# Seven-product up-projections on one core: split order, places, squares and token sums rearranged

## The chip, the core and the metric

The kernel runs on one core of one Trainium2 chip. The metric is the device time of one execution in microseconds (us); the number of a kernel is the median of its runs. TensorE (PE) does the matmuls, VectorE (DVE), ScalarE (ACT) and GpSimd (POOL) the elementwise work, and SyncE (SP) issues most transfers. Each engine works through its own list of instructions in order and waits on semaphores of the others.

## The reference, cut to what matters

The whole program is a chain of layers over 512 tokens of width 1024, in single precision. The change concerns the two squared-ReLU MLPs (width 4096):

```python
def sqrelu_mlp(h, w_up, w_down):
    u = jax.nn.relu(h @ w_up)
    return (u * u) @ w_down

def first_block(...):
    for i in range(DEPTH):                       # DEPTH = 2
        h = rms_norm(x, mixer_norm[i])
        ...                                      # attention (i = 0), rwkv (i = 1)
        x = x + sqrelu_mlp(rms_norm(x, mlp_norm[i]), mlp_w_up[i], mlp_w_down[i])
    return rms_norm(x, final_norm)
```

After them come two SwiGLU layers and a mixer, which the change does not touch.

## The kernel before

Activations lie as eight tiles `x[m]` of 128 features x 512 tokens. A single-precision product is made of three fast ones (`mm3`, lines 454 to 456): every operand is split into a high part `hi`, written by ACT as a rounded copy, and a low part `lo = t - hi`, written by DVE; then hi*hi, hi*lo and lo*hi are summed in PSUM. So each half of a weight unit (128 x 512) costs ACT one copy and DVE one subtraction before PE can use it. Below, "a split" is that pair of instructions, lines 230 and 232 for the up-projections treated here, 241 and 242 for all other weights.

**The MLP** (`mlp`, line 577) goes through the 32 blocks of 128 hidden features in 4 groups of 8. In a group the up-projections are done first, in 4 pairs of blocks, then the down-projections of the 8 blocks are added into `x`. The first two pairs of the first group are plain products (`product`, 128x512 matmuls). The other 14 pairs of each MLP use `product7` (line 513): the 2x2 block scheme with seven products in place of eight. The four blocks are two halves of the input features by two output blocks for the weights, and by two halves of the tokens for the activations. A product is 4 x 3 = 12 matmuls of 128x256, so a pair is 84. PE does the products in the order P1, P2, P6, P5, P7, P3, P4. P1, P6, P7 and P4 are summed into one PSUM bank (`a`), P2 into one half of another and P5, P3 into its other half; between the products ACT copies running sums out of PSUM: into `c1` after P1 (line 535) and P6 (540), into `c2` after P5 (543) and P7 (546). The next product into the same place has to wait for that copy.

**Weights** (`Weights`, line 86). Raw weights come in units of 512 KB through a ring of three tiles (`wraw`); a pair takes two units, `a` = (a11, a21) and `b` = (a12, a22). Four of the seven products take sums of these as weights; `sums` makes them in place on DVE (lines 170, 173, 175, 177). A split goes into a "place" of one of two pools with 6 places each: `wsplit` for P1, P2, P3 and for all other weights, `w7` for the products named in `SUMS`. `ahead` is called after each product and goes on splitting, in the order of `SPLIT_ORDER`, until the next one in that order finds its own pool full (`can`). When the last use of a raw unit is split (`LAST`), the next unit is fetched into its tile.

**Activations for the seven products** (`open_seven`, `sums`, line 488) are token sums of `x[q]` and `x[q+4]`, q = 0 to 3, each scaled by the norm's gain: ACT makes one 128x256 product, DVE three scalar_tensor_tensor operations, then ACT and DVE split the results into `x7`. They are called behind k = 7 of the first plain product and k = 1, 3, 5 of the second. The first plain product also carries the norm's statistics: sums by PE at k = 4, a chain of small operations on ACT and DVE, and at k = 6 four transposes by PE (line 436) of its result `sy`.

**After the products** (`put`, line 602): DVE adds `c2` (line 608) or the bank (617) to the running sum, takes the ReLU with the norm's factor (line 600, tile `t`), ACT squares it twice (lines 594, 595: rounded `uh`, exact `u`) and DVE makes `ul` (597). Both squares of a pair stand on ACT ahead of the next pair's first copy. Order on each engine is simply the order in which this code issues.

## Time and profile before

| what | value |
|---|---|
| median of 3 runs | 2666.29 us (2663.71 to 2667.12) |
| the profiled execution | 2659.23 us, span on the core 2657.3 us |
| PE busy | 2328.1 us, 88% of the span |
| DVE, ACT, POOL busy | 1576.2, 1104.9, 426.7 us |
| mean granted TensorE clock | 0.933 of full |

The profile is of one execution, taken instruction by instruction. A row of its timeline gives start and length in us, engine, source line, operation, and in brackets how long the engine had been idle just before and what ended that. TensorE's clock has two levels, 1.2 and 2.4 GHz; the profile calls them 0.5 and 1.0.

### The profile page before, as it was taken

To read this page: it belongs to the slowest core of one execution; us is meant where nothing else is said; L and a number is where in the kernel's file an instruction comes from. 1 tells how busy PE (TensorE), PEld (TensorE's weight loads), DVE (VectorE), ACT (ScalarE), POOL (GpSimd) and SP (SyncE) were. 2 spreads that over 40 slices of the span, in tenths; PEclk is the share of its full clock that TensorE was granted. 3 is DMA by queue.
4 is the path that set the end of the run, shared out by engine and by line. 5 is a ranking of instruction groups with operands and counts; after the bars stand their busy time and mean duration, and the time that the engine had idled before them with its cause. 6 is when DMAs were issued, how large, how long until landed. Compare 5 with 4: busy or idle time off the path is not lost. (4 is left out here: it accounts for less than half of the span.)

```text
span 2657.3 us, 36157 instructions
## 1 busy us (share of the span) xinstructions
PE 2328.1 (88%) x13828; PEld 1958.0 (74%) x13828; DVE 1576.2 (59%) x2847; ACT 1104.9 (42%) x2107; POOL 426.7 (16%) x430
## 2 busy tenths in 40 slices
PE   8889686977887879895977869999998999899997
PEld 6678576777765766775777767888886888688886
DVE  7987654545578883766545555535346764744445
ACT  5476433333356445433333334333234554433222
POOL 3753000000136452220000002000003002200002
PEclk9999898989999988997988979999999999999999
DMA  4321121212232447531222212222322312232322
GB/s 150 103 60 40 48 95 64 80 65 79 99 97 83 123 136 195 174 112 55 80 71 73 87 57 88 88 96 95 103 81 69 118 61 85 80 102 91 100 92 68
DMA packets 105340, 241.95 MB, mean 91 GB/s; under 512 B 18120, under 2 KB 36936, under 8 KB 105168
## 3 DMA queue, kind: packets, MB, share of 16 engines
q1 hardware_dynamic: 102976, 234.46, 27.5%
q0 software_dynamic: 1040, 3.51, 0.4%
q8 instruction: 109, 1.79, 0.3%
q10 hardware_dynamic: 1152, 1.68, 0.2%
q14 instruction: 63, 0.52, 0.1%
HBM read 214.62 MB, written 19.22 MB: 88 GB/s over the span
## 5 line engine op out<-in xcount | busy, mean ns | idle before, releaser
L454 PE MATMUL mm<-xh,whi 128*128 128x512 f32 (+4 forms) x2056 | 763.4, 371 | 209.4 <-ACT c L535 142.2
L455 PE MATMUL mm<-xl,whi 128*128 128x512 f32 (+4 forms) x2056 | 750.7, 365 | 10.8 <-DVE xl L364 9.5
L456 PE MATMUL mm<-xh,wlo 128*128 128x512 f32 (+4 forms) x2056 | 747.6, 364 | 9.0 <-DVE wlo L242 9.0
L242 DVE TENSOR_TENSOR wlo<-wraw,whi 128x512 fp32r<-128x512 f32 (+2 forms) x590 | 438.4, 763 | 443.6 <-ACT whi L241 430.9
L454 PEld LDWEIGHTS mm<-xh,whi 128*128 128x128 f32 (+3 forms) x2056 | 416.6, 203 | 273.6 <-ACT c L535 146.3
L241 ACT CAST whi<-wraw 128x512 fp32r<-128x512 f32 (+3 forms) x609 | 360.5, 611 | 456.6 <-PE mm L455 388.1
L455 PEld LDWEIGHTS mm<-xl,whi 128*128 128x128 f32 (+3 forms) x2056 | 416.8, 203 | 66.9 <-DVE xl L364 15.0
L456 PEld LDWEIGHTS mm<-xh,wlo 128*128 128x128 f32 (+3 forms) x2056 | 414.9, 202 | 65.4 <-DVE wlo L242 11.8
L454 PE MATMUL mm<-uh,whi 128*128 128x512 f32 (+1 forms) x900 | 347.5, 386 | 0.0
L456 PE MATMUL mm<-uh,wlo 128*128 128x512 f32 (+1 forms) x900 | 347.2, 386 | 0.0
L455 PE MATMUL mm<-ul,whi 128*128 128x512 f32 (+1 forms) x900 | 347.2, 386 | 0.0
L380 POOL TENSOR_TENSOR acc<-acc,sq 128x512 f32<-128x512 f32 (+1 forms) x55 | 73.6, 1337 | 1676.0 <-ACT sq L379 1236.5
L456 PEld LDWEIGHTS mm<-uh,wlo 128*128 128x128 f32 x900 | 169.2, 188 | 37.4
L454 PEld LDWEIGHTS mm<-uh,whi 128*128 128x128 f32 x900 | 169.2, 188 | 37.0
L455 PEld LDWEIGHTS mm<-ul,whi 128*128 128x128 f32 x900 | 169.2, 188 | 37.0
L230 ACT CAST whi<-wraw 128x512 fp32r<-128x512 f32 x168 | 99.3, 619 | 101.6 <-DMA wraw<-in_up 25.6
L232 DVE TENSOR_TENSOR wlo<-wraw,whi 128x512 fp32r<-128x512 f32 x168 | 112.8, 688 | 12.7 <-ACT whi L230 8.9
L608 DVE TENSOR_TENSOR c<-c 128x256 f32<-128x256 f32 x28 | 11.9, 425 | 169.4 <-ACT c L546 169.4
L654 DVE TENSOR_TENSOR x<-mm,x 128x512 f32<-128x512 f32 x64 | 44.1, 690 | 74.0 <-PE mm L456 73.7
L594 ACT ACTIVATE uh<-t 128x512 fp32r<-128x512 f32 x64 | 40.1, 627 | 90.5 <-DVE t L600 90.5
L363 ACT ACTIVATE xh<-x,vec 128x512 fp32r<-128x512 f32 (+1 forms) x50 | 35.2, 705 | 82.7 <-DVE x L702 22.0
L597 DVE TENSOR_TENSOR ul<-u,uh 128x512 fp32r<-128x512 f32 x64 | 44.1, 688 | 30.2 <-ACT u L595 30.2
(538 smaller groups left out, 3246.1 us busy)
## 6 DMA issues: line engine op xcount, KB each, us to landing
wraw<-in_ffn_in SPq DMA_DIRECT2D x88, 512.0 KB, 3.8
wraw<-in_up SPq DMA_DIRECT2D x64, 512.0 KB, 4.2
wraw<-in_down SPq DMA_DIRECT2D x64, 512.0 KB, 3.8
wraw<-in_rwkv SPq DMA_DIRECT2D x34, 512.0 KB, 5.0
wraw<-in_ffn_out SPq DMA_DIRECT2D x32, 512.0 KB, 3.7
wraw<-in_mix SPq DMA_DIRECT2D x32, 512.0 KB, 3.8
wraw<-in_dsa SPq DMA_DIRECT2D x23, 512.0 KB, 3.7
wraw<-in_ffn_out SPq DMA_DIRECT2D x16, 384.0 KB, 3.0
```

The lines of the kernel that those rows point to most:

```text
L230: self.nc.scalar.copy(hi, t)
L232: self.nc.vector.tensor_sub(lo, t, hi.bitcast(F32))
L241: self.nc.scalar.copy(hi[:, :per], t)
L242: self.low.tensor_sub(lo[:, :per], t, hi[:, :per].bitcast(F32))
L363: nc.scalar.activation(hi, x, AF.Copy, scale=gm)
L380: (low or (nc.vector if m == NB - 1 else nc.gpsimd)).tensor_add(acc, acc, q[:, s])
L454: nc.tensor.matmul(ps, w[0], x[0], start=start, stop=False, **how)
L455: nc.tensor.matmul(ps, w[0], x[1], start=False, stop=False, **how)
L456: nc.tensor.matmul(ps, w[1], x[0], start=False, stop=stop, **how)
L594: nc.scalar.activation(hi, t, AF.Square)
L597: return lambda: nc.vector.tensor_sub(lo, u, hi.bitcast(F32))
L654: nc.vector.tensor_add(self.x[m], p, self.x[m])
```

## The change

- `SPLIT_ORDER` becomes the order in which PE uses the products. `SUMS` goes; a split of a seven-product weight takes a place in either pool, `w7` first (`room`, `can`, `split_one`). The sum for P7 is made together with that for P6; the first raw unit is now free after P7.
- `put` no longer issues squares at once. The squares of the first result (`t1`, from P3) follow P4; those of the second (`t`) follow the next pair's copy behind P1 (`put(2, ...)`), and its `ul` the next pair's P2 (`put(3, ...)`). At a group's end `rest` issues what is left.
- The token sums: ACT scales both whole tiles (two 128x512), GpSimd makes four subtractions of 128x256 in place, and the split of each q is issued one call later. The calls move to k = 1, 3, 5, 7 of the first plain product; the last split to k = 0 of the second.

```diff
-SPLIT_ORDER = ("P1", "P7", "P2", "P6", "P5", "P3", "P4")
-SUMS = ("P7", "P5", "P6", "P4")
+SPLIT_ORDER = ("P1", "P2", "P6", "P5", "P7", "P3", "P4")
...
-LAST = dict(P5=0, P4=1)
+LAST = dict(P7=0, P4=1)
...
-    def pool(self, j):
-        return self.halves[j][1] in SUMS
...
+    def room(self, p):
         used = self.used.setdefault(p, [])
         n = self.seven_bufs if p else self.bufs
         return len(used) < n or used[-n] not in self.parts
 
+    def can(self, j):
+
+        if j >= len(self.halves):
+            return False
+        if isinstance(self.halves[j][1], int):
+            return self.room(False)
+        return bool(self.seven) and (self.room(True) or self.room(False))
...
-        if c == "P7":
+        if c == "P6":
             v.tensor_sub(a21, a11, a21)
-        elif c == "P6":
             self.s2 = self.scratch.tile([128, 512], F32, name="s2")
             v.tensor_sub(self.s2, a22, a21)
...
-        p = self.pool(self.done)
+        p = not isinstance(h, int) and self.room(True)
         pool = self.seven if p else self.split
...
         def sums(q, g, pair):
...
+            if q < 4:
+                a, b = pair()
+                y = [a, b]
+                for i in range(2):
+                    nc.scalar.activation(y[i], self.x[q + 4 * i], AF.Copy, scale=g[:, q + 4 * i:q + 4 * i + 1])
+                (b11, b12), (b21, b22) = ((t[:, first], t[:, s]) for t in y)
+
+                nc.gpsimd.tensor_sub(b11, b12, b11)
+                nc.gpsimd.tensor_sub(b12, b22, b12)
+                nc.gpsimd.tensor_sub(b22, b22, b11)
+                nc.gpsimd.tensor_sub(b21, b21, b22)
+            while low:
+                low.pop()()
...
+                def split():
+                    for t, (hi, lo) in zip(y, tiles):
+                        nc.scalar.copy(hi, t)
+                        nc.vector.tensor_sub(lo, t, hi.bitcast(F32))
+                low.append(split)
...
         run("P1", a, True)
         nc.scalar.copy(plus[:, first], a)
+        put(2, 0, None, None)
         self.w.ahead()
         run("P2", b, True)
+        put(3, 0, None, None)
         self.w.ahead()
...
             def put(i, h, p, plus):
 
-                if i == 2:
-                    later.pop()()
+                if i > 1:
+                    for f in later.pop(i, ()):
+                        f()
                     return
+                if plus is not None:
+                    nc.vector.tensor_add(plus, p, plus)
                 if i and h:
...
                 elif i:
-                    relu(later[0], p, HALVES[0])
-                    t, low = later
-                    later[:] = [square(t)]
-                    low()
+                    low = square(later.pop("t1"))
+                    t = later.pop("t")
+                    relu(t, p, HALVES[0])
+                    later[2] = [lambda: later.update({3: [square(t)]}), low]
                 else:
...
-                    later.append(square(t))
+                    later["t1"] = tp.tile([128, T], F32, name="t")
+                    relu(later["t1"], plus)
...
             def beside(k):
                 self.stats_beside(k)
-                if k == 7:
-                    sums_at(0)
+                if k % 2:
+                    sums_at(k // 2)
```

Line numbers move: 230 and 232 become 227 and 229, 535/540/543/546 become 535/542/545/548, 608 and 617 become 610, 600 becomes 601, 594 to 597 become 595 to 598, and 170/173/175/177 become 168/170/172/174.

ACT, first MLP, second group, from the end of the first pair into the second. Before, from the last split ahead of the squares:

```order
L230 CAST whi_3940<-wraw_3919 128x512
L594 ACTIVATE uh_3962<-t_3959 128x512
L595 ACTIVATE u_3961<-t_3959 128x512
L594 ACTIVATE uh_3980<-t_3912 128x512
L595 ACTIVATE u_3979<-t_3912 128x512
L230 CAST whi_3985<-s2_3943 128x512
L535 COPY c1_3993<-mm_3991 128x256
L540 COPY c1_3993<-mm_3991 128x256
L543 COPY c2_3994<-mm_3992 128x256
L546 COPY c2_3994<-mm_3991 128x256
L230 CAST whi_4062<-wraw_3782 128x512
```

The same place after:

```order
L227 CAST whi_3968<-wraw_3762 128x512
L595 ACTIVATE uh_3985<-t_3966 128x512
L596 ACTIVATE u_3984<-t_3966 128x512
L227 CAST whi_3990<-wraw_3762 128x512
L535 COPY c1_3999<-mm_3997 128x256
L595 ACTIVATE uh_4015<-t_3946 128x512
L596 ACTIVATE u_4014<-t_3946 128x512
L227 CAST whi_4020<-wraw_3858 128x512
L227 CAST whi_4037<-wraw_3858 128x512
L542 COPY c1_3999<-mm_3997 128x256
L227 CAST whi_4056<-wraw_3893 128x512
L545 COPY c2_4000<-mm_3998 128x256
```

The squares of `t` (here from `t_3946`) have moved behind the copy of line 535, and a split now stands between each two copies, where before the four copies stood in a row.

DVE, same group, first pair, from the sum on `c2` on. Before:

```order
L608 TENSOR_TENSOR c2_3846<-c2_3846 128x256
L600 SCALAR_TENSOR_TENSOR t_3912<-c2_3846,rs_70 128x256
L177 TENSOR_TENSOR wraw_3760<-wraw_3760,s2_3822 128x512
L232 TENSOR_TENSOR wlo_3915<-wraw_3758,whi_3914 128x512
L232 TENSOR_TENSOR wlo_3922<-wraw_3760,whi_3921 128x512
L232 TENSOR_TENSOR wlo_3926<-wraw_3760,whi_3925 128x512
L170 TENSOR_TENSOR wraw_3782<-wraw_3782 128x512
L232 TENSOR_TENSOR wlo_3932<-wraw_3782,whi_3931 128x512
L232 TENSOR_TENSOR wlo_3937<-wraw_3782,whi_3936 128x512
L173 TENSOR_TENSOR s2_3943<-wraw_3919,wraw_3782 128x512
L232 TENSOR_TENSOR wlo_3941<-wraw_3919,whi_3940 128x512
L617 TENSOR_TENSOR c1_3845<-mm_3844,c1_3845 128x512
```

After:

```order
L229 TENSOR_TENSOR wlo_3926<-wraw_3858,whi_3925 128x512
L610 TENSOR_TENSOR c2_3852<-c2_3852 128x256
L601 SCALAR_TENSOR_TENSOR t_3946<-c2_3852,rs_70 128x256
L172 TENSOR_TENSOR wraw_3762<-s2_3929,wraw_3762 128x512
L229 TENSOR_TENSOR wlo_3949<-s2_3929,whi_3948 128x512
L610 TENSOR_TENSOR c1_3851<-mm_3850,c1_3851 128x512
L601 SCALAR_TENSOR_TENSOR t_3966<-c1_3851,rs_70 128x512
L229 TENSOR_TENSOR wlo_3969<-wraw_3762,whi_3968 128x512
L601 SCALAR_TENSOR_TENSOR t_3946<-mm_3849,rs_70 128x256
L174 TENSOR_TENSOR wraw_3858<-wraw_3858,s2_3929 128x512
L229 TENSOR_TENSOR wlo_3991<-wraw_3762,whi_3990 128x512
L598 TENSOR_TENSOR ul_3986<-u_3984,uh_3985 128x512
```

Nine instructions for weights stood between the two sums on `c`; two are left there, and the weight work is spread over the pair.

DVE, first MLP, first plain product, around the norm's statistics. Before, from the end of the chain that makes `sy`:

```order
L399 SCALAR_TENSOR_TENSOR sy_3029<-stt_3030,sy_3029 128x4
L438 COPY rs_70<-st_3049 128x512
L491 TENSOR_SCALAR ng_2974<-vec_66 128x8
L497 SCALAR_TENSOR_TENSOR t_3062<-x0_72,ng_2974,t_3062 128x256
L499 SCALAR_TENSOR_TENSOR u_3063<-x4_76,vec_66,t_3062 128x512
```

After, up to the beginning of that chain (`sv`):

```order
L170 TENSOR_TENSOR s2_3036<-wraw_3026,wraw_3020 128x512
L229 TENSOR_TENSOR wlo_3033<-wraw_3026,whi_3032 128x512
L172 TENSOR_TENSOR wraw_3020<-s2_3036,wraw_3020 128x512
L229 TENSOR_TENSOR wlo_3040<-s2_3036,whi_3039 128x512
L229 TENSOR_TENSOR wlo_3045<-wraw_3020,whi_3044 128x512
L174 TENSOR_TENSOR wraw_3026<-wraw_3026,s2_3036 128x512
L229 TENSOR_TENSOR wlo_3049<-wraw_3020,whi_3048 128x512
L229 TENSOR_TENSOR wlo_3058<-wraw_3026,whi_3057 128x512
L509 TENSOR_TENSOR xl0_3001<-t_2992,xh0_3000 128x512
L509 TENSOR_TENSOR xl1_3003<-u_2993,xh1_3002 128x512
L386 TENSOR_SCALAR sv_3088<-st_3083 128x4
```

The splits of the first seven-product pair, which came behind the plain products' results, and the split of q = 0 now stand ahead of the statistics' chain; the first of them reads raw unit `b` (`wraw_3026`).

## Rows read from the trace of the kernel before

**Rows 1.** The page, busy time of the matmul engine: us, share, instructions.
```profile
PE 2328.1 (88%) x13828; PEld 1958.0 (74%) x13828; DVE 1576.2 (59%) x2847; ACT 1104.9 (42%) x2107; POOL 426.7 (16%) x430
```

**Rows 2.** The waits: who waited for whom; us in total, times, longest.
```profile
PE mm L454 <- ACT c L535: 142.2, 20, 8.0
...
PE mm L454 <- issue: 42.4, 2, 21.2
```

**Rows 3.** Stretches: length, busy time of each engine, granted clock, DMA; up-projections.
```profile
298.50:352.90 54.40, 25.68 (x170) 25.30 (x169) 31.85 (x54) 20.90 (x41) 0.00 (x0) 0.69 0.17 58
397.60:465.70 68.10, 47.20 (x338) 46.58 (x337) 34.17 (x58) 24.52 (x50) 0.00 (x0) 0.82 0.19 62
...
1208.90:1261.70 52.80, 23.98 (x170) 23.57 (x170) 31.91 (x54) 21.00 (x41) 0.00 (x0) 0.74 0.18 60
...
sum 518.50, PE 333.94 PEld 329.42 DVE 268.98 ACT 189.00 POOL 0.00; mean PE 41.74 PEld 41.18 DVE 33.62 ACT 23.62 POOL 0.00
```

**Rows 4.** Stretches behind two idle times of PE, same columns.
```profile
417.40:420.40 3.00, 2.97 (x14) 2.97 (x15) 1.04 (x2) 0.00 (x0) 0.00 (x0) 0.50 0.00 0
420.40:429.10 8.70, 8.66 (x72) 8.45 (x71) 5.14 (x9) 3.92 (x8) 0.00 (x0) 1.00 0.18 54
1152.90:1154.40 1.50, 0.00 (x0) 0.00 (x0) 1.48 (x3) 0.00 (x0) 0.00 (x0) 1.00 0.95 279
1154.40:1164.40 10.00, 9.96 (x55) 8.78 (x56) 6.76 (x9) 5.79 (x10) 2.31 (x2) 1.00 0.58 197
```

**Rows 5.** Timeline of PE, second pair of a group: P6 starts.
```profile
417.43 0.58 PE L454 MATMUL mm<-xh,whi 128*128 128x256 f32 x1 [6.77 <-ACT c L535]
```

**Rows 6.** Timeline of ACT, the same place.
```profile
414.41 0.63 ACT L594 ACTIVATE uh<-t 128x512 fp32r<-128x512 f32 x1 [2.09 <-DVE t L600]
...
416.51 0.60 ACT L230 CAST whi<-s 128x512 fp32r<-128x512 f32 x1
417.02 0.36 ACT L535 COPY c<-mm 128x256 f32<-128x256 f32 x1
```

**Rows 7.** Timeline of DVE, the pair before that place.
```profile
405.36 0.42 DVE L608 TENSOR_TENSOR c<-c 128x256 f32<-128x256 f32 x1 [6.89 <-ACT c L546]
...
411.71 0.69 DVE L173 TENSOR_TENSOR s<-wraw 128x512 f32<-128x512 f32 x1 [0.91 <-DMA wraw<-in_up]
...
413.69 0.69 DVE L600 SCALAR_TENSOR_TENSOR t<-c,rs 128x512 f32<-128x512 f32 x1
```

**Rows 8.** Timeline of the SP queue: the fetch of that raw unit.
```profile
407.47 1.92 SPq L186 DMA_DIRECT2D wraw<-in_up  x2
```

**Rows 9.** Timeline of PE, first MLP: transposes of the statistics; first P6.
```profile
285.76 0.60 PE L436 MATMUL st<-con,sy 128*128 128x128 f32 x4
...
322.62 0.55 PE L454 MATMUL mm<-xh,whi 128*128 128x256 f32 x1 [21.12 <-issue]
```

**Rows 10.** Timeline of the SP queue there: fetch of unit b and the next.
```profile
281.48 1.24 SPq L186 DMA_DIRECT2D wraw<-in_up  x2
```

**Rows 11.** Timeline of DVE there: statistics, then sums and splits of the first pair.
```profile
283.12 0.16 DVE L389 TENSOR_SCALAR sv<-st 128x4 f32<-128x4 f32 x1 [0.98 <-PE st L418]
...
284.16 0.16 DVE L399 SCALAR_TENSOR_TENSOR sy<-stt,sy 128x4 f32<-128x4 f32 x1
...
296.08 0.68 DVE L170 TENSOR_TENSOR wraw<-wraw 128x512 f32<-128x512 f32 x1
...
301.67 0.48 DVE L497 SCALAR_TENSOR_TENSOR t<-x,ng,t 128x256 f32<-128x256 f32 x1
```

**Rows 12.** Groups of instructions by shape: count, busy us, mean ns, idle before.
```profile
L363 ACT ACTIVATE xh<-x,vec 128x512 fp32r<-128x512 f32 x46 | 33.2, 722 | 82.0 <-DVE x L702 21.4 <-DVE x L1108 20.0 <-DVE x L654 19.0
...
L380 POOL TENSOR_TENSOR acc<-acc,sq 128x256 f32<-128x256 f32 x6 | 4.5, 744 | 15.3 <-ACT sq L379 15.3
```

**Rows 13.** Timelines of POOL and DVE: an add of POOL beside two subtractions.
```profile
259.69 1.34 POOL L380 TENSOR_TENSOR acc<-acc,e 128x512 f32<-128x512 f32 x1 [3.83 <-ACT e L379]
...
260.09 2.09 DVE L242 TENSOR_TENSOR wlo<-wraw,whi 128x512 fp32r<-128x512 f32 x2 [0.21 <-ACT whi L241]
```

More of the change, by code (lines that the diff above doesn't have):

```diff
@@ L138, in close_seven @@
         self.seven = None
-    def pool(self, j):
-        return self.halves[j][1] in SUMS
+    def room(self, p):
+        used = self.used.setdefault(p, [])
+        n = self.seven_bufs if p else self.bufs
+        return len(used) < n or used[-n] not in self.parts
     def can(self, j):
@@ L146, in can @@
             return False
-        p = self.pool(j)
-        if p and not self.seven:
-            return False
-        used = self.used.setdefault(p, [])
-        n = self.seven_bufs if p else self.bufs
-        return len(used) < n or used[-n] not in self.parts
+        if isinstance(self.halves[j][1], int):
+            return self.room(False)
+        return bool(self.seven) and (self.room(True) or self.room(False))
     def sums(self, j):
@@ L158, in sums @@
         u, c = self.halves[j]
-        if c not in ("P7", "P6", "P5", "P3") or not self.seven:
+        if c not in ("P6", "P5", "P3") or not self.seven:
             return
@@ L484, in open_seven @@
         self.x7 = [None] * (NB // 2)
-        ng = self.small.tile([128, NB], F32, name="ng")
         first, s = HALVES
+        low = []
         def sums(q, g, pair):
-            if q == 0:
-                nc.vector.tensor_scalar(ng, g, -1.0, None, op0=OP.mult)
-            (x11, x12), (x21, x22) = ((self.x[q + 4 * i][:, first], self.x[q + 4 * i][:, s]) for i in range(2))
-            g1, g2 = (g[:, q + 4 * i:q + 4 * i + 1] for i in range(2))
-            a, b = pair()
-            t1, y = a[:, first], a[:, s]
-            nc.scalar.activation(y, x12, AF.Copy, scale=g1)
-            nc.vector.scalar_tensor_tensor(t1, x11, ng[:, q:q + 1], y, op0=OP.mult, op1=OP.add)
-            two = [t.rearrange("p (i t) -> p i t", i=2) for t in (b, a)]
-            nc.vector.scalar_tensor_tensor(two[0], x22[:, None, :].to_broadcast([128, 2, 256]), g2, two[1],
-                                           op0=OP.mult, op1=OP.subtract)
-            nc.vector.scalar_tensor_tensor(y, x21, g2, b[:, first], op0=OP.mult, op1=OP.subtract)
-            tiles = []
-            for i, t in enumerate((a, b)):
-                hi, lo = (pool.tile([128, T], F32R, name=f"x{n}{2 * q + i}") for n in "hl")
-                nc.scalar.copy(hi, t)
-                nc.vector.tensor_sub(lo, t, hi.bitcast(F32))
-                tiles.append((hi, lo))
-            self.x7[q] = {p: [t[:, h] for t in tiles[i]] for p, i, h in
-                          (("P5", 0, first), ("P4", 0, s), ("P6", 1, first), ("P7", 1, s))}
@@ new lines, in sums @@
+            while low:
+                low.pop()()
+            if q < 4:
+                tiles = [[pool.tile([128, T], F32R, name=f"x{n}{2 * q + i}") for n in "hl"] for i in range(2)]
+                self.x7[q] = {p: [t[:, h] for t in tiles[i]] for p, i, h in
+                              (("P5", 0, first), ("P7", 0, s), ("P6", 1, s), ("P4", 1, first))}
+                def split():
[3 more added lines that the diff above has]
+                low.append(split)
@@ L554, in product7 @@
         self.w.ahead()
-        put(2, 0, None, None)
     def part(self, p, w, c, x, s, k, K, free):
@@ L630, in mlp @@
             for g in range(nff // G):
-                us, later = [], []
+                us, later = [], {}
                 for f in range(0, G, 2):
                     if g == 0 and f < 4:
-                        ps = self.product(xg, n=2, hook=(beside, lambda k: k in (1, 3, 5) and sums_at(k // 2 + 1))[f // 2])
+                        ps = self.product(xg, n=2, hook=(beside, lambda k: k == 0 and sums_at(4))[f // 2])
                         for p in ps:
@@ L640, in mlp @@
                         self.product7(xg, put)
+                rest()
                 last = g == nff // G - 1
```

11 lines of the change are left out of this document (5 added, 6 removed).

## The prediction

> **What bounds the kernel now.** I read the page first: PE is busy 88% of the span [rows 1], so the kernel is bound by PE, and the time to be had is where PE stands still or runs at the lower clock. The waits say where: PE waited 20 times, 142.2 us in all, for the copy of line 535, and twice, 42.4 us, where no single releaser shows ("issue") [rows 2]. All of these are in the up-projections. The view by stretches gives these their size: the eight stretches of seven-product pairs, 28 pairs, take 518.5 us [rows 3]. At the 2.4 GHz level 72 matmuls take 8.66 us, 0.12 each [rows 4], so a pair of 84 would be 10.1 us and all 28 would be 282 us. 236 us are lost there.
>
> The second step is why. PE stands before P6 of a pair until 417.43, 6.77 us, for the copy of line 535, though P1, whose result is copied, had long ended [rows 5]. The copy ran at 417.02 and took 0.36: it stood in ACT's list behind a split (416.51) and four squares (from 414.41), and these waited 2.09 us for DVE's ReLU [rows 6]. DVE came to that ReLU (413.69) so late because it had been idle for 6.89 us until 405.36, waiting for the copy out of `c`, with all splits of the next pair queued behind that wait; it then did them in one piece, and stood once more for raw weights that landed at 411.71 [rows 7], 4.24 us after their fetch was issued at 407.47 [rows 8]. So PE and DVE work in turns: while PE does P6, P5, P7, DVE waits; while DVE catches up, PE waits. Each such wait costs more than itself: PE came back at the 1.2 GHz level, 14 matmuls in 2.97 us, 0.21 each [rows 4]. The 21.12 us before the first P6 of the first MLP [rows 9] are of the same kind: DVE works through splits, token sums and ReLUs in a row, of which the second set of token sums begins only at 301.67 [rows 11].
>
> **The change part by part.**
>
> *Splits in product order, any place.* With 12 places in one order each release frees the next place, so ahead of each product stand up to 12 split halves, 1.7 pairs, and each release asks for one split: DVE's work is spread over the pair. Does it fit? DVE's instructions follow one another at 0.62 us when 512 wide (nine in the 5.59 us from 296.08 to 301.67 [rows 11]). A pair is 4 sums, 7 splits and 2 `ul`, 13 x 0.62 = 8.1; two wide ones on the first result at 0.7 = 1.4; three half-wide ones at 0.42 [rows 7] = 1.3: 10.7 us against PE's 10.1. But 12 of a group's 28 splits are done beside the down-projections, and the stretch of a group holds only 34.2 us of DVE work today [rows 3], against 4 x 10.1 = 40.3 of PE. It fits, with little air in the pairs in the middle.
>
> *What is late next: the fetch.* Unit `b` of the next pair but one can be fetched when P7 of the next pair is split, which in ACT's new list stands behind the squares of this pair's `t1`. From one pair's squares to the next pair's I count: two squares 1.05 and a split 1.25; the fetch 4.24 [rows 7, 8]; then on DVE two sums and two splits 2.5, the two half-wide ones on `c2` 0.84 and the two on `c1` 1.4. That is 11.3 us, 1.2 more than PE's pair. It bites only where both the fetch and its use fall inside a group: the first pair's unit was fetched at the group's start, the last pairs need none. So once in full per group, 1.2 us; with hand-overs that I can't see in rows of before I take 2.0, bounds 0 and 3 x 1.2 = 3.6. Waits of this length need not cost the clock: PE was idle 1.5 us at 1152.9 and the granted clock stayed at 1.0 after it [rows 4].
>
> *Squares behind the copy.* At the copy of line 535 ACT now has before it two squares and one split, 1.05 + 0.6 us after P4 if DVE's ReLU is in time, and PE needs the copy only after P1 and P2, 2.9 us. So the copy is hidden. If DVE is 1.3 us late, PE waits from there on; that is the 1.2 above. The moved squares stand ahead of P2's split and the copy of line 542, which PE needs 1.4 us after P6; ACT's work in a pair is 24.52/4 = 6.1 us [rows 3], so it has room.
>
> *One group* of four pairs is then 40.3 + 2.0 = 42.3 us. The six whole groups take 518.5 - 54.4 - 52.8 = 411.3 us now [rows 3]; 6 x 42.3 = 253.8. **Gain 157.5 us.**
>
> *Entry of each MLP.* The token sums leave DVE three scalar operations for each q (some 1.7 us), 7 us in all, put two 0.72 us scalings on ACT in place of one half-wide one, and 4 subtractions on POOL at about 0.74 [rows 12], 3.0 us for each q, with POOL otherwise idle. But the order also puts the first pair's splits ahead of the statistics, and they need unit `b`, whose fetch is issued at 281.48 [rows 10] and lands near 285.7. Then come 8 instructions of DVE at 0.62 (to 290.7), on ACT two scalings and one split (to some 292.2), two subtractions on DVE (293.5), and the small chain, 1.2 us with its square root from 283.12 to 284.32 [rows 11]; with ACT's table load between, 295.0. PE does the transposes at 285.76 now [rows 9], so here it gets a new wait of 9.3 us. POOL's sums for q = 1 run beside those two subtractions and may hold them up: 0 to 3 us, I take 2, so 11 in all. In exchange the 21 us before the first P6 shrink: behind the transposes PE has 12.7 us of plain products (285.76 to 298.5) and P1, P2, 2.9 us, and in these 15.6 us DVE's six open splits of token sums (3.7 us) fit beside the first ReLUs; what is left is the copy of line 535 behind the second plain pair's ReLUs and squares, about 3 us (twice ReLU, squares and hand-over, 1.3 + 1.05 + 0.6, with two splits, less the 2.9 of P1 and P2). Group 1 of an MLP: wait 11, lower clock after it 2.2 (between 3.0 us of it [rows 4] and twice that, half of it lost), two pairs 20.2, copy 3, rest 0.4: 36.8, against 54.4 and 52.8. **Gain 33.6 us for both.**
>
> On POOL beside DVE the rows show: two subtractions of DVE took 2.09 us beside an add of POOL [rows 13], where two in a row take 1.3 [rows 11]. The Trainium skill, SBUF — State Buffer, section "Who interferes with whom", says that a VectorE instruction with two SBUF inputs and a GpSimd instruction that reads SBUF exclude each other for their whole length; the trace agrees, with 0.8 us. By that rule the 12 us of POOL's sums would be taken from DVE in full, and that speaks against this part of the change.
>
> *Sum.* Against the profiled execution: span 2657.3 - 157.5 - 33.6 = 2466; with the 1.9 us around it 2468. The median of the runs stands 7.1 above the profiled one: **2475 us**.
>
> **The rivals.**
> - *The waits only shrink.* If the fetch takes 6 us under load or hand-overs add 2 us, the loop of 11.3 becomes over 13, and DVE, with 10.7 us of work, can't make it up; three pairs of each group wait some 3 us, and the clock falls for 3.0 us each time, 1.5 lost: 18 x 4.5 = 81, less the 12 already counted: 2544. For it: DVE and ACT both stood for weights [rows 7]. Against: those fetches are one pair ahead in two of four cases.
> - *POOL holds DVE up in full.* All 12 us of sums on the path of each MLP in place of 2: 2 x 10 more, 2495. Against: only q = 1 lies in the chain; the others have slack.
> - *The change doesn't do what it says*: a place is asked for in one list but freed late, the copy still waits behind splits, and the 20 waits stay. Then the groups keep 411 us and the entries give or take a few: 2640 to 2670.
> - *Slower: PE stays at 1.2 GHz.* If a wait comes in every pair and the clock doesn't return in between, a pair is 84 x 0.21 = 17.9 plus 2 of waiting, 28 of them 557 us, 38 more than now, and the two new waits at the statistics add 22: 2726. It decides from about 18.5 us for a pair, today's mean. Against: after 6.77 us of idling the clock was back within 3.0 us and stayed for at least 8.7 [rows 4].
>
> **How the numbers follow.** Forecast 0.65 (2445 to 2515), shrunken waits 0.20, POOL 0.09, no effect 0.03, slower 0.03. The range runs from 2445, where neither the entry's wait nor the loop appears (2666 - 236 = 2430 is the floor), to 2550, which takes in the first two rivals. A measurement of this kernel can tell about 0.2% from no change. Faster by more: 0.65 + 0.20 + 0.09 and a third of the no-effect case, 0.95; within: 0.02; slower: 0.03.
>
> **What would show it.** Right: the waits of PE for line 535's copy gone or under 2 us; group stretches near 42 us with the clock near 1.0; DVE no longer idle before line 610; a new wait of PE of 9 to 12 us at the transposes, and ACT and DVE there waiting for the fetch of `in_up`. Wrong: stretches over 50 us, waits of ACT for raw weights of several us in each pair, or a lower clock through whole groups.

## The result, and the profile after

| | kernel before | changed kernel |
|---|---|---|
| median of 4 runs each, us | 2665.24 | 2469.79 |
| lowest to highest | 2663.71 to 2667.12 | 2466.48 to 2470.97 |
| span of the profiled execution, mean granted clock | 2657.3, 0.933 | 2464.7, 0.962 |

The changed kernel takes 0.9264 of the time of the one before, with a 95% interval of 0.9248 to 0.9280: 195 us less, against a forecast of 2475.

The engines' line of the page after, which answers to [rows 1]: PE is busy 93% of the span in place of 88%, GpSimd has 32 instructions more.

```profile
PE 2282.1 (93%) x13828; PEld 1917.9 (78%) x13828; DVE 1560.8 (63%) x2821; ACT 1105.2 (45%) x2115; POOL 454.0 (18%) x462
```

The stretches of the up-projections after (length; busy time of PE, weight load, DVE, ACT and POOL with their instructions; granted clock, share of DMA, GB/s), which answer to [rows 3]. All eight sum to 305.40 us where they were 518.50. The six whole groups take 42.0 us each at a clock of 1.00, and DVE does its 34 us of work in 42 where it had 68.

```profile
311.40:338.90 27.50, 22.87 (x170) 22.70 (x169) 17.00 (x30) 13.16 (x27) 0.00 (x0) 0.88 0.20 69
382.80:424.80 42.00, 40.63 (x338) 40.23 (x337) 33.94 (x58) 24.50 (x51) 0.00 (x0) 1.00 0.32 103
...
1130.20:1156.10 25.90, 21.56 (x170) 21.36 (x169) 16.50 (x29) 13.02 (x27) 0.00 (x0) 0.93 0.22 76
...
sum 305.40, PE 287.82 PEld 285.00 DVE 237.17 ACT 173.27 POOL 0.00; mean PE 35.98 PEld 35.62 DVE 29.65 ACT 21.66 POOL 0.00
```

The waits after (who for whom: us in total, times, longest), which answer to [rows 2]: the 142.2 us of line 535 are 12.9, the 42.4 us without a releaser are 4.6, and the new wait at the transposes stands there twice. DVE's own wait for the copy out of `c` (line 610, before the change line 608) went from 169.4 us to 25.6; the first row is of the kernel before, the others of the changed one. What is left of it is 5.0 and 3.9 us at the two entries and 1.2 to 1.6 us twice in each whole group.

```profile
DVE c L608 <- ACT c L546: 169.4, 28, 6.9
```

```profile
PE st L433 <- DVE sy L396: 19.6, 2, 10.0
...
DVE c L610 <- ACT c L548: 25.6, 16, 5.0
...
PE mm L451 <- ACT c L535: 12.9, 13, 4.3
...
PE mm L451 <- issue: 4.6, 1, 4.6
```

The entry of the first MLP after, from the timelines of PE, of the SP queue, of ACT and of DVE. PE stands 10.03 us before the transposes. At that time ACT and DVE stand for the raw weights that SP fetched at 282.14 and that landed 4.7 us later, and DVE then does the first pair's splits ahead of the small chain. The second wait, 4.63 us, is before the first P6.

```profile
296.59 1.09 PE L433 MATMUL st<-con,sy 128*128 128x128 f32 x4 [10.03 <-DVE sy L396]
...
318.95 0.55 PE L451 MATMUL mm<-xh,whi 128*128 128x256 f32 x1 [4.63 <-issue]
```

```profile
282.14 1.24 SPq L183 DMA_DIRECT2D wraw<-in_up  x2
```

```profile
286.83 0.62 ACT L227 CAST whi<-wraw 128x512 fp32r<-128x512 f32 x1 [4.25 <-DMA wraw<-in_up]
```

```profile
286.90 0.69 DVE L170 TENSOR_TENSOR s<-wraw 128x512 f32<-128x512 f32 x1 [2.92 <-DMA wraw<-in_up]
```

### The profile page after: what moved, and what is told of

The parts are those of the page before. It is cut to its first block, busy times and chain, and to the rows that moved or that the text cites. A ratio compares the mean times of both kernels' runs of the same rounds, so it can differ in the third digit from the quotient of the medians.

```text
span 2464.7 us, 36301 instructions
## 1 busy us (share of the span) xinstructions
PE 2282.1 (93%) x13828; PEld 1917.9 (78%) x13828; DVE 1560.8 (63%) x2821; ACT 1105.2 (45%) x2115; POOL 454.0 (18%) x462
## 5 line engine op out<-in xcount | busy, mean ns | idle before, releaser
L451 PE MATMUL mm<-xh,whi 128*128 128x512 f32 (+4 forms) x2056 | 743.7, 362 | 44.8 <-ACT c L535 12.9
L452 PE MATMUL mm<-xl,whi 128*128 128x512 f32 (+4 forms) x2056 | 733.1, 357 | 10.7 <-DVE xl L361 9.7
L453 PE MATMUL mm<-xh,wlo 128*128 128x512 f32 (+4 forms) x2056 | 731.9, 356 | 10.8 <-DVE wlo L239 10.8
L451 PEld LDWEIGHTS mm<-xh,whi 128*128 128x128 f32 (+3 forms) x2056 | 397.0, 193 | 107.7 <-issue 24.5
L453 PEld LDWEIGHTS mm<-xh,wlo 128*128 128x128 f32 (+3 forms) x2056 | 396.0, 193 | 68.6 <-DVE wlo L239 14.4
L452 PEld LDWEIGHTS mm<-xl,whi 128*128 128x128 f32 (+3 forms) x2056 | 396.9, 193 | 67.0 <-DVE xl L361 15.7
L452 PE MATMUL mm<-ul,whi 128*128 128x512 f32 (+1 forms) x900 | 342.2, 380 | 0.0
L808 ACT CAST uh<-a 128x512 fp32r<-128x512 f32 x44 | 27.3, 621 | 76.5 <-DVE a L807 76.5
L361 DVE SCALAR_TENSOR_TENSOR xl<-x,vec,xh 128x512 fp32r<-128x512 f32 (+1 forms) x50 | 44.0, 884 | 24.7 <-ACT xh L360 24.4
```

The costliest lines, as they stand in the source:

```text
L361: nc.vector.scalar_tensor_tensor(lo, x, gm, hi.bitcast(F32), op0=OP.mult, op1=OP.subtract)
L451: nc.tensor.matmul(ps, w[0], x[0], start=start, stop=False, **how)
L452: nc.tensor.matmul(ps, w[0], x[1], start=False, stop=False, **how)
L453: nc.tensor.matmul(ps, w[1], x[0], start=False, stop=stop, **how)
```

## The experiments

Each kernel ran beside the kernel before on the same chip, and its time is given as the ratio to it. Chips differ a little (the kernel before had medians of 2659 to 2665 us), so kernels from different sets are compared by these ratios; the changed kernel's is 0.9264.

### One part of the change at a time

Theory: PE and DVE worked in turns because of the order of the splits, and the squares ahead of the copy of line 535 came on top. Rival: one of the two alone was the cause. Three kernels carry one part each: `w_only` the new split order and places (class Weights; the two were not separated), `sq_only` the new place of the squares (`put`, `rest` and the two calls in `product7`), `tok_only` the token sums (`open_seven`, `beside` and the hook).

The lines that make them out, of `w_only`, `sq_only` and `tok_only` in turn:

```diff
-SPLIT_ORDER = ("P1", "P7", "P2", "P6", "P5", "P3", "P4")
+SPLIT_ORDER = ("P1", "P2", "P6", "P5", "P7", "P3", "P4")
...
+        return bool(self.seven) and (self.room(True) or self.room(False))
```

```diff
         run("P1", a, True)
         nc.scalar.copy(plus[:, first], a)
+        put(2, 0, None, None)
         self.w.ahead()
         run("P2", b, True)
+        put(3, 0, None, None)
```

```diff
+                nc.gpsimd.tensor_sub(b11, b12, b11)
+                nc.gpsimd.tensor_sub(b12, b22, b12)
+                nc.gpsimd.tensor_sub(b22, b22, b11)
+                nc.gpsimd.tensor_sub(b21, b21, b22)
...
-                if k == 7:
-                    sums_at(0)
+                if k % 2:
+                    sums_at(k // 2)
```

> The kernel before with the splits in product order into any free place, and nothing else of the change. Theory 1 (the splits are what made PE and DVE work in turns): DVE is in time again, and the copy of the first result still stands behind four squares and one split, about 1 us more than P1 and P2 take; a group of four pairs then takes 44 to 48 us, the six of them 265 to 290 in place of 411, and the time is 2525 to 2550 us. Theory 2 (the squares ahead of that copy are the cause by themselves): the copy is as late as before, groups stay above 60 us, time above 2600. Both: at the entry of each MLP a wait of about 10 us at the transposes of the statistics appears, since it comes from the splits of the first pair standing ahead of them.

> The kernel before with the squares moved behind the next copy, and nothing else of the change. Theory 1: PE's wait before P6 for the copy goes down, but DVE still does its splits in one piece behind the wait for c22, so PE waits for split weights instead; groups of 58 to 66 us, time 2600 to 2650. Theory 2: the squares alone were the cause; groups of 45 us or less, time below 2540.

> The kernel before with the token sums on GpSimd from the first plain product on, and nothing else of the change. Both theories: the six whole groups keep 411 us; only the two entries move. Theory 1: the wait of 21 us before the first P6 shrinks by some 8 us in each MLP, since about 7 us of DVE's token sums leave the path, and no wait of 10 us appears at the transposes, because the splits of the first pair are not ahead of them; time 2645 to 2655. Rival: GpSimd's sums hold DVE up in full, 12 us for each MLP, and the time is 2665 or more.

| kernel | ratio (95%) | median, us | six whole groups, us |
|---|---|---|---|
| w_only | 0.9615 (0.9594 to 0.9637) | 2559.22 | 326.6 |
| sq_only | 0.9852 (0.9824 to 0.9879) | 2619.98 | 375.8 |
| tok_only | 0.9927 (0.9908 to 0.9946) | 2640.87 | 412.4 |
| all three | 0.9264 (0.9248 to 0.9280) | 2469.79 | 252.4 |

The groups took 411.3 us before. The splits alone win 84.7 there, the squares alone 35.5, both 158.9: 38.7 more than the two together. Neither is the cause by itself. `w_only` missed its number (I expected 265 to 290 us): in a group PE waits three times for the copy, 8.3 us in all, and in the 3 us behind each the granted clock is 0.50 to 0.58. The timelines of PE, ACT and DVE in the middle of a group of that kernel show why the copy is late.

```profile
405.53 0.58 PE L451 MATMUL mm<-xh,whi 128*128 128x256 f32 x1 [3.06 <-ACT c L532]
```

```profile
400.80 0.63 ACT L591 ACTIVATE uh<-t 128x512 fp32r<-128x512 f32 x1 [3.13 <-DVE t L597]
...
401.86 0.60 ACT L227 CAST whi<-wraw 128x512 fp32r<-128x512 f32 x1
403.55 0.63 ACT L591 ACTIVATE uh<-t 128x512 fp32r<-128x512 f32 x1 [1.09 <-DVE t L597]
...
405.12 0.36 ACT L532 COPY c<-mm 128x256 f32<-128x256 f32 x1
```

```profile
402.49 0.69 DVE L229 TENSOR_TENSOR wlo<-wraw,whi 128x512 fp32r<-128x512 f32 x1 [1.73 <-ACT whi L227]
403.10 0.42 DVE L597 SCALAR_TENSOR_TENSOR t<-mm,rs 128x256 f32<-128x256 f32 x1
```

In each pair ACT's squares wait for a ReLU, a split stands behind the squares, DVE's low half behind that split (1.73 us idle), the next ReLU behind the low half, the next squares behind that ReLU, and only then comes the copy. Moving the squares cuts this chain, but only if the splits are spread; in `sq_only` DVE still stands idle for the copy out of `c` and then does everything in one piece, as in [rows 7], and PE waits 5.49 us, still for the copy of line 535 and not for split weights as I expected:

```profile
401.31 0.43 DVE L610 TENSOR_TENSOR c<-c 128x256 f32<-128x256 f32 x1 [6.89 <-ACT c L548]
```

```profile
412.11 0.58 PE L454 MATMUL mm<-xh,whi 128*128 128x256 f32 x1 [5.49 <-ACT c L535]
```

`tok_only` left the groups alone, as both theories said; the first P6 of the first MLP waited 11.92 us in place of 21.12 [rows 9], and no wait came at the transposes (0.67 us). Some 10 of its 18 us are another thing (the last experiment below). `w_only` has the wait at the transposes, 7.0 and 6.15 us where I expected about 10, so it does come with the new split order.

### The wait at the transposes: does it cost 10 us?

Theory: the splits of the first pair, ahead of the statistics in the lists, cost PE those 10 us. Rival: DVE and ACT are late with the whole entry, and the wait only shows where PE meets that. `a_hold` holds the first pair's splits back until the transposes are issued; `a_late` leaves them and takes only the second plain pair's squares from in front of line 535; `a_best` and `a_best4` hold the splits back and reorder the entry further.

Of `a_hold` (`hold` is set where the MLP begins), `a_late`, `a_best` and `a_best4` in turn:

```diff
-        return bool(self.seven) and (self.room(True) or self.room(False))
+        return not self.hold and bool(self.seven) and (self.room(True) or self.room(False))
...
+                if k == 6:
+                    self.w.hold = False
+                    self.w.ahead()
```

```diff
-                            square(t)()
+                            if f:
+                                later[2 + i] = [lambda t=t: square(t)()]
+                            else:
+                                square(t)()
```

```diff
+                if k == 7:
+                    self.w.hold = False
+                    self.w.ahead()
+                    sums_at(4)
...
+                        if f == 0:
+                            for low in [square(t) for t in ts]:
+                                low()
+                        else:
+                            self.w.hold = True
+                            later[2] = [lambda ts=ts: later.update(l=square(ts[0]))]
+                            later[3] = [lambda ts=ts: [low() for low in (later.pop("l"), square(ts[1]))]]
```

```diff
+                                lows.append(square(t))
+                                if len(lows) == 1:
+                                    self.w.hold = False
+                                    self.w.ahead(3)
+                                    self.w.hold = True
+                                    sums_at(4)
...
+                        self.product7(xg, put, 2 if g == 0 and f == 4 else None)
```

> The kernel after, with the splits of the first seven-product pair held back until the transposes of the statistics have been issued (in both MLPs). Theory 1: the 10 us wait of PE at the transposes is the wait of DVE's list for the fetch and eight instructions of splits ahead of the statistics; with these behind, the transposes run at once, the splits fit beside the 12.7 us of plain products, and each MLP gains 6 to 9 us: 2452 to 2458. Rival: DVE's work at the entry is what counts, the wait only moves to the first P6, time 2466 to 2472.

> The kernel after, with the squares of the second plain pair (ahead of the first seven-product pair of each MLP) put behind the copy of line 535, as the change does for the other pairs. Theory (ACT's list is what holds the copy there): of PE's wait before the first P6, 4.6 and 4.3 us in the kernel after, nothing is left, since the copy then stands behind a split that ran at 311.6 and PE needs it at 314.3; the 10 us at the transposes stay; 9 us less in all, 2457 to 2462. Rival (DVE is behind with its work at the entry, and who waits for it doesn't matter): the wait goes to a later product, time 2466 to 2472.

> The kernel after with its entry reordered in three ways: splits of the first seven-product pair held back until the last plain step of the first plain pair; both ReLUs of a plain pair ahead of its squares, so that DVE doesn't stand 1.2 us before each of four low parts; the second plain pair's squares, and the splits of the second seven-product pair, behind the copy of line 535. Theory (the entry is bound by DVE's and ACT's lists, 14.6 us of PE's idle time that the held splits alone only moved from the transposes to the first P6): no wait at the transposes, 2 to 4 us before the first P6, some 10 us less in each MLP, time 2445 to 2452. Rival: DVE's sheer work at the entry is the bound, the 14 us stay, 2465 to 2472.

> The kernel after with its entry written in another order. First ReLU and squares of the first plain pair, then the splits of P1, P2 and P6 alone, the last token sums, the second ReLU and squares, both low parts; the second plain pair's squares and all further splits behind the copy of line 535, and from there two splits for each product of the first seven-product pair. Theory (PE's 14.6 us of idle time at the entry come from the order of DVE's and ACT's lists): no wait at the transposes, under 2 us before the first P6 and before P7, entry and first group of an MLP 47 to 50 us where the kernel after has 63, time 2438 to 2446. Rival (DVE's sheer work there is the bound): the waits come back before later products, 2455 or more.

| kernel | ratio (95%) | median, us | entry and first group, first MLP, us | PE's waits over 1 us in it |
|---|---|---|---|---|
| changed | 0.9264 (0.9248 to 0.9280) | 2469.79 | 63.1 | 10.03, 4.63 |
| a_hold | 0.9260 (0.9244 to 0.9276) | 2462.92 | 60.4 | 13.84 |
| a_late | 0.9218 (0.9202 to 0.9233) | 2456.52 | 56.8 | 9.93 |
| a_best | 0.9218 (0.9204 to 0.9232) | 2457.21 | 56.2 | 6.36, 2.47 |
| a_best4 | 0.9233 (0.9219 to 0.9247) | 2457.02 | 58.0 | 1.05, 2.32, 5.68 |

The timeline of PE in `a_hold`, `a_best` and `a_best4` in turn:

```profile
314.32 0.55 PE L452 MATMUL mm<-xh,whi 128*128 128x256 f32 x1 [13.84 <-issue]
```

```profile
306.23 0.55 PE L452 MATMUL mm<-xh,whi 128*128 128x256 f32 x1 [6.36 <-issue]
313.11 0.58 PE L452 MATMUL mm<-xh,whi 128*128 128x256 f32 x1 [2.47 <-ACT c L544]
```

```profile
306.29 0.38 PE L452 MATMUL mm<-xh,whi 128*128 128x256 f32 x1 [1.05 <-ACT whi L228]
313.17 0.39 PE L452 MATMUL mm<-xh,whi 128*128 128x256 f32 x1 [2.32 <-ACT c L547]
325.37 0.58 PE L452 MATMUL mm<-xh,whi 128*128 128x256 f32 x1 [5.68 <-ACT c L536]
```

My theory fell with `a_hold`: the wait at the transposes was gone, and nearly as many microseconds stood before the first P6, 13.84 where the two waits together had 14.66. (The times of the entry are of one profiled execution each; in `a_swap`, `a_pool` and `a_ng`, which leave the entry alone, it took 61.7 to 62.3 us, so the 60.4 of `a_hold` is hardly a gain.) `a_best` and `a_best4` missed their numbers too: I expected 2445 to 2452 and 2438 to 2446 us. Of the squares it held: `a_late` takes the 4.63 us away, and with them the lower clock behind them; its first group takes 20.89 us at 1.00 (stretch of the two pairs in `a_late`):

```profile
309.87:330.76 20.89, 20.26 (x170) 20.06 (x169) 16.28 (x29) 12.52 (x27) 0.00 (x0) 1.00 0.28 87
```

With those squares moved, some 9 us of waiting stay in each order that I tried (9.93; 8.83; 9.05); they only change their place. The stretch of `a_best` from its second set of token sums to the second wait points to the reason: DVE is busy for 25.65 of 28.80 us while PE has 20 us of work.

```profile
285.00:313.80 28.80, 19.97 (x105) 17.50 (x104) 25.65 (x37) 16.95 (x32) 6.63 (x7) 0.86 0.16 52
```

That DVE's work is the floor there is argued from this row; a kernel with less work at that place was not run. `a_late` and `a_best` both beat the changed kernel, their intervals lie below its own; `a_late` does it with one edit.

### The wait of 1 us in each group

Once in each whole group PE waits 1.03 to 1.17 us for line 535. The prediction put it down to a loop over the fetch of unit `b`; a rival is DVE's list, which is nearly full there. First the loop, from the timelines of SP, ACT, DVE and PE of the changed kernel:

```profile
396.52 0.54 SPq L183 DMA_DIRECT2D wraw<-in_up  x1
```

```profile
394.11 0.63 ACT L595 ACTIVATE uh<-t 128x512 fp32r<-128x512 f32 x1 [1.23 <-DVE t L601]
...
400.62 0.62 ACT L227 CAST whi<-wraw 128x512 fp32r<-128x512 f32 x1 [0.92 <-DMA wraw<-in_up]
...
405.42 0.63 ACT L595 ACTIVATE uh<-t 128x512 fp32r<-128x512 f32 x1 [1.25 <-DVE t L601]
...
406.48 0.60 ACT L227 CAST whi<-wraw 128x512 fp32r<-128x512 f32 x1
406.99 0.36 ACT L535 COPY c<-mm 128x256 f32<-128x256 f32 x1
```

```profile
400.77 0.69 DVE L170 TENSOR_TENSOR s<-wraw 128x512 f32<-128x512 f32 x1
...
404.69 0.69 DVE L601 SCALAR_TENSOR_TENSOR t<-c,rs 128x512 f32<-128x512 f32 x1
...
407.11 0.69 DVE L229 TENSOR_TENSOR wlo<-wraw,whi 128x512 fp32r<-128x512 f32 x1 [0.19 <-ACT whi L227]
```

```profile
407.40 0.39 PE L451 MATMUL mm<-xh,whi 128*128 128x256 f32 x1 [1.04 <-ACT c L535]
```

From the fetch at 396.52 to its use at 400.6 are 4.1 us; DVE's eight instructions from 400.77 to the end of the wide ReLU at 405.38 are 4.6; squares, split and low half, which frees the raw place again, end at 407.80: 11.3 us in all, as from squares to squares (394.11 to 405.42). `a_nosum` leaves out one DVE instruction of each pair that is not in this loop (the sum of line 174, so that P3 is made with another operand); `a_swap` asks for the splits ahead of the squares behind the copy; `a_pool` gives one low part of each pair to GpSimd.

In turn:

```diff
-            v.tensor_sub(a12, a12, self.s2)
+            pass
```

```diff
         nc.scalar.copy(plus[:, first], a)
+        self.w.ahead()
         put(2, 0, None, None)
+        run("P2", b, True)
         self.w.ahead()
-        run("P2", b, True)
         put(3, 0, None, None)
-        self.w.ahead()
```

```diff
-            def square(t):
+            def square(t, eng=nc.vector):
...
-                    low = square(later.pop("t1"))
+                    low = square(later.pop("t1"), nc.gpsimd)
```

> The kernel after without the third sum of the weights (line 174, one instruction of 0.6 us on DVE in each pair), so that the product P3 is made with another operand. Nothing else moves: the fetch of the raw weights, the squares and the splits keep their order. Theory 1 (DVE's list is the loop: in the middle pairs of a group it worked 10.6 of 11.3 us): the wait of 1.04 us once in each group falls to half or less, groups of 41.2 to 41.6 us, 3 to 5 us less in all. Theory 2, that of the prediction (the loop runs over squares, split, fetch and the sums behind it, and this instruction isn't in it): groups stay at 42.1 us.

> The kernel after, with the splits asked for ahead of the deferred squares behind the copies of lines 535 and behind P2, so that the split which frees a raw place runs one pair of squares, 1.05 us, earlier. Theory (the wait of 1.04 us once in each group is the loop over the fetch: squares, split, fetch, sums): the wait goes, groups of 41.0 us in place of 42.1, time 6 us less. Rival (it is the order of work on ACT, not the fetch): the squares are now late, and groups stay or grow; no gain.

> The kernel after, with the low part of the first square of each seven-product pair made by GpSimd in place of DVE (line 598). Theory 1 (DVE's list bounds the middle pairs): DVE has 0.6 us less in each pair but its instructions beside GpSimd's take 0.3 to 0.5 us longer, one or two of them; groups of 41.6 to 42.1 us, 0 to 3 us less. Rival (GpSimd takes its whole time, 1.3 us, from DVE): groups of 42.8 us, 4 us more.

`a_nosum` ran at 0.9274 (0.9259 to 0.9288), and its groups stayed at 42.1 us but for one of 42.9: what DVE had less to do became idle time, and PE waited as before (timelines of DVE and PE). DVE's load is not what sets the wait; the prediction's theory stands.

```profile
403.64 0.69 DVE L229 TENSOR_TENSOR wlo<-wraw,whi 128x512 fp32r<-128x512 f32 x1 [0.79 <-ACT whi L227]
```

```profile
403.93 0.39 PE L451 MATMUL mm<-xh,whi 128*128 128x256 f32 x1 [1.03 <-ACT c L535]
```

`a_swap` ran at 0.9259 (0.9245 to 0.9273), the same as the changed kernel, with the 1.07 us still there. What I expected of it was wrong, for a reason of the code: it moves the squares behind the copy, and the squares in the loop are those of `t1`, which stand ahead of the copy in both kernels (405.42 above). So `a_swap` leaves the loop untested. `a_pool` ran at 0.9287 (0.9274 to 0.9301), with groups of 42.7 us, 0.6 more than the changed kernel: the rival's number, but not its reason, since DVE lost 0.8 of GpSimd's 1.41 us each time.

What `a_pool` does show is the loop. GpSimd's instruction holds up the low half that frees the raw place: 1.49 us in place of 0.69. The fetch of the next unit then begins 3.2 us after the squares (390.73 to 393.94) where the changed kernel has 2.4 (394.11 to 396.52), DVE stands 0.70 us for these weights, and from squares to squares it is 11.97 us in place of 11.31. The rows are of ACT and DVE in `a_pool`:

```profile
390.73 0.63 ACT L595 ACTIVATE uh<-t 128x512 fp32r<-128x512 f32 x1 [1.23 <-DVE t L601]
...
402.70 0.63 ACT L595 ACTIVATE uh<-t 128x512 fp32r<-128x512 f32 x1 [1.25 <-DVE t L601]
```

```profile
392.42 1.49 DVE L229 TENSOR_TENSOR wlo<-wraw,whi 128x512 fp32r<-128x512 f32 x1 [0.20 <-ACT whi L227]
...
398.05 0.69 DVE L170 TENSOR_TENSOR s<-wraw 128x512 f32<-128x512 f32 x1 [0.70 <-DMA wraw<-in_up]
```

A later fetch made the loop longer; no run made the fetch shorter.

### GpSimd beside DVE

`a_dve` puts the sixteen subtractions of the token sums on DVE.

```diff
-                nc.gpsimd.tensor_sub(b11, b12, b11)
...
+                nc.vector.tensor_sub(b11, b12, b11)
...
```

> The kernel after, with the sixteen subtractions of the token sums of each MLP on DVE in place of GpSimd. Theory 1 (as the trace of the kernel after shows single instructions: DVE's take 1.0 to 1.2 us beside GpSimd in place of 0.68, some six of them on the path): DVE has 16 x 0.42 = 6.7 us more work in each MLP and saves some 3, most of it on the path; 2 to 4 us slower in each MLP, time 2473 to 2478. Rival (GpSimd's 12 to 15 us are taken from DVE in full): DVE's own sums are shorter, 5 us faster in each MLP, time 2458 to 2464.

It ran at 0.9269 (0.9255 to 0.9283), no different from the changed kernel, and entry and first group took 63.1 us in both: neither number came. The timelines tell why both could miss. First of GpSimd and DVE in the changed kernel at the entry, then of the same two in `a_pool`:

```profile
292.94 0.72 POOL L495 TENSOR_TENSOR t<-u,t 128x256 f32<-128x256 f32 x1
293.74 1.05 POOL L496 TENSOR_TENSOR u<-u,t 128x256 f32<-128x256 f32 x1
```

```profile
293.20 1.00 DVE L509 TENSOR_TENSOR xl<-t,xh 128x512 fp32r<-128x512 f32 x1 [1.05 <-ACT xh L508]
294.13 1.21 DVE L509 TENSOR_TENSOR xl<-u,xh 128x512 fp32r<-128x512 f32 x1
```

```profile
403.93 1.41 POOL L598 TENSOR_TENSOR ul<-u,uh 128x512 fp32r<-128x512 f32 x1 [10.56 <-ACT u L596]
```

```profile
404.39 1.50 DVE L229 TENSOR_TENSOR wlo<-wraw,whi 128x512 fp32r<-128x512 f32 x1 [0.19 <-ACT whi L227]
```

They take turns, instruction by instruction. GpSimd's first ends at 293.66, and DVE's, begun at 293.20, ends 0.54 later, at 294.20; GpSimd's second, begun at 293.74, ends 0.59 after that, at 294.79; DVE's second 0.55 after that. In `a_pool` DVE's ends 0.55 after GpSimd's end at 405.34. Two in a row on DVE are 0.6 apart, so DVE simply waited out GpSimd; and GpSimd, whose instruction takes 0.73 us alone, waited out DVE. The Trainium skill, SBUF — State Buffer, section "Who interferes with whom", says that a VectorE instruction with two SBUF inputs contends with a GpSimd instruction that reads SBUF, by an exclusive lock; the traces agree. But the price is not GpSimd's whole time. Of its 14.0 us in the first MLP only 6.2 lie beside a DVE instruction of this kind. There six of its own sixteen instructions wait for DVE (1.05 to 1.23 us in place of 0.73), and what DVE's five instructions lost is 2.3 us (0.32 + 0.53 + 0.32 + 0.54 + 0.55). On DVE the sums cost sixteen times 0.42, but save this loss and the hand-overs between the two engines (1.05 us before 293.20). The two came out even.

### The down-projections: 64 bytes

Nothing of the change is in the down-projections, yet their stretches fell, in the layers that the change doesn't touch too. The prediction had nothing of it. The changed kernel has lost one small tile, `ng`, 128 x 8 floats in two buffers, 64 bytes of each partition, and all tiles allocated behind it on that side of SBUF lie 64 bytes lower (by the order of allocation in the code). `a_ng` allocates it again, unused.

```diff
+        self.small.tile([128, NB], F32, name="ng")
         first, s = HALVES
         low = []
```

> The kernel after, with the small tile ng put back (128 x 8 floats in two buffers, 64 bytes in each partition, which nothing reads or writes), so that all tiles allocated behind it, those of the squares among them, have the addresses of the kernel before again. Not one instruction changes. Theory (the down-projections got 0.8 us faster in each stretch because their moving operand, uh and ul, lies 64 bytes lower): the down-projection stretches are 44.8 to 45.0 us again in place of 44.1, in the untouched layers too, and the time is 8 to 12 us more, 2476 to 2482. Rival (the change of instructions, or the one profiled execution, did it): stretches of 44.1 and no change of time.

It ran at 0.9307 (0.9291 to 0.9322), above the changed kernel by 0.43% of the time before, some 11 us: the theory's number. The same stretch, a down-projection of the first MLP, in the kernel before, the changed kernel and `a_ng`:

```profile
465.52:510.48 44.96, 44.96 (x196) 36.20 (x195) 24.99 (x40) 15.68 (x26) 0.00 (x0) 1.00 0.28 94
```

```profile
424.69:468.81 44.12, 44.12 (x196) 36.22 (x195) 24.44 (x39) 14.89 (x26) 0.00 (x0) 1.00 0.28 95
```

```profile
422.48:467.44 44.96, 44.96 (x196) 36.20 (x195) 24.46 (x39) 14.89 (x26) 0.00 (x0) 1.00 0.29 97
```

Not one instruction differs between the last two, and the clock is 1.00 in all. `w_only` and `sq_only`, which keep the tile, have 44.96 too (in the second MLP 44.8, as the kernel before); every kernel without it, `tok_only` among them, has 44.1. So it is the place of tiles in SBUF, not the instructions around. Which tile matters was not separated: the squares `uh` and `ul` are read as moving operand there, and the places of the weights split for the plain products, allocated from the other side, did not move.

## Why the prediction was right, step by step

- **The six groups: right, by the mechanism given.** 253.8 us predicted, 252.4 measured. The wait that I took at 2.0 us was 1.03 to 1.17, and my count of the loop, 1.2, was nearer than what I took. The loop of 11.3 us is there, with the members that the prediction listed; `a_nosum` shows that it is not DVE's load, and in `a_pool` a later fetch made the loop longer. Of the signs named, one came only in part: DVE still waits before line 610, 25.6 us in place of 169.4.
- **What the two parts are worth: not said.** The prediction costed the groups as one. The runs show that the splits win 123.4 us in the groups with the squares moved and 84.7 without, the squares 74.2 with the new splits and 35.5 without.
- **The wait at the transposes: right in size, wrong in what it costs.** 11 us predicted, 10.03 and 9.54 measured, with ACT and DVE waiting for the fetch as said. The prediction called it a price of the new split order. The wait does come with that order (`w_only` has it, `tok_only` not), but `a_hold` shows that it is not a price: without it the time stays, since PE then waits later.
- **The rest of the entry: the term mis-sized.** Group 1 with its waits was 36.8 in the sum. In the first MLP it was 39.9: waits of 10.03 and 4.63, 2.15 and 2.9 lost to the lower clock behind each (half of the stretches below), and 20.2 for two pairs. In the second it was 38.1. I had taken 3 us for the copy of line 535 and no lower clock behind it. So the entries won 29.3 us in place of 33.6. The stretches behind the two waits, at a clock of 0.51 and 0.50:

```profile
296.60:300.90 4.30, 4.30 (x13) 3.54 (x14) 2.79 (x4) 3.33 (x7) 4.01 (x5) 0.51 0.00 0
...
318.90:324.70 5.80, 5.75 (x27) 5.78 (x28) 2.48 (x4) 1.76 (x4) 0.00 (x0) 0.50 0.47 160
```

- **GpSimd beside DVE.** I took 2 us of the path for each MLP, and the rival with all 12 us of it 2495. The exclusion is whole, as the rival had it, but DVE lost only 2.3 us by it in the first MLP: less than half of GpSimd's time lies beside an instruction of DVE that it excludes, and there GpSimd waits as well as DVE. So the rival's price didn't come.
- **What was missing.** The down-projections gave 10.2 us that no step of mine had. On the other side the stretch between the two MLPs, where nothing is changed, took 418.1 us before and 421.9 after; in the other kernels it took 420.5 to 427.4, so I make nothing of it. In the profiled executions the sum is 158.9 for the groups, 29.3 for the entries, 10.2 for the down-projections, less 5.8 elsewhere: 192.6, the difference of the spans.
- **The sum fits better than its steps.** The span came to 2464.7 where the sum had 2466: the groups' 1.4 us and the unforeseen 10.2 on the one side, the entries' 4.3 and the 5.8 elsewhere on the other. That these cancel is luck. Most of the 5 us between forecast and median is another term: I took the median to stand 7.1 us above the profiled execution, and it stood 3.3 above (2469.79 against 2466.48).

## What to carry to other kernels

Where two engines work in turns, ask for the whole cycle of hand-overs: one edit that cuts one link may give a fraction of what two give together. A wait that one can name is not yet a price: hold back what it waits for, and see whether the time goes or only moves. And when a change adds or drops a small tile, compare a stretch that it doesn't touch before explaining the rest.

## What the runs showed of the hardware

A shift of 64 bytes in the place of SBUF tiles changed the down-projections' stretches of 196 matmul records from 44.12 to 44.96 us, 1.9%, at the same granted clock, while stretches of plain products of 87.2 us stayed as they were. GpSimd and DVE subtractions that both read two SBUF operands excluded each other: DVE's ended 0.54 to 0.55 us after GpSimd's end, where two in a row on DVE are 0.60 apart, and GpSimd's ended 0.59 us after DVE's, where it takes 0.73 alone. PE's idle times of 1.03 to 1.17 us in the groups left the granted clock at 1.00. One of 2.32 us in a group of `w_only` (before 435.44) was followed by 3.06 us at 0.50, the lower of the two levels; one of 2.32 us in `a_best4` (before 313.17) by 2.9 us at 1.00.
